# Attention maxima of seven heads: from columns to rows by single-element DMAs instead of matmuls, and a pair of PSUM evacuations on one engine

## The chip, the cores and the metric

One Trainium2 chip, of which the kernel uses one core. The metric is the device time of one execution in microseconds, as the median of several runs.

## What is computed

One layer for a prompt of 1024 tokens and a sample of 64 tokens that follow a cache of 256; the model is 1024 wide and all numbers are float32. After an input projection there are two groups of heads: eight attention heads, 64 wide, whose scores carry a sum of log-forget values, and four heads, 128 wide, with a gated linear recurrence. Both are gated, joined, projected to the output and normalised. The attention of one head:

```
s = einsum('bqhd,bkhd->bhqk', q, k) * 64 ** -0.5
s = s + (c_q[..., :, None] - c_k[..., None, :])      # c = cumsum(logf)
s = where(mask, s, -inf)
p = softmax(s, axis=-1)                              # subtracts each query's maximum
return einsum('bhqk,bkhd->bqhd', p, v)
```

The subtraction of the maximum inside the softmax is where the change lies.

## The kernel before

Matrix products run in a 32-bit format with fewer mantissa bits (`fp32r`), so each operand is split into a high and a low part, and a product is made of two or three.

**Stages.** In the trace the start (projection of the values and of the forget gate) takes the first 81 us. From 81 to 337 us the eight attention heads are worked one after another, here numbered 0 to 7 in their order (four pairs, `s` = 0 and 1 within a pair). Between their steps stands the "filler": projections of later stages, cut into pieces, which `merge` deals out by estimated cost (ratio `RA`). From 337 to 600 us the recurrence runs, again with projections between its steps, and from 600 us the output projection. TensorE (PE) does the matmuls, ScalarE (ACT) exponentials and copies, VectorE (DVE) maxima, masks and subtractions, GpSimd (POOL) low parts, and SyncE (SP) issues nearly all DMAs, in one queue in order.

**One head.** The 1024 queries are worked in two chunks of 512. For a block of 128 keys `scores` makes two matmuls into one bank of PSUM (L811, L812): the first of `QX` and `KX`, the second of `QY` and `KY`, whose extra rows carry the forget sums and the negated maximum. ACT takes the exponential twice (L817, L818), DVE subtracts for the low part (L819), and `values` multiplies with V (L836, three matmuls). The sample of 64 queries is worked in `attend_sample` between the steps of the second chunk.

**The maximum as a row.** The maximum of each query must stand in rows 2 and 3 of a small block of `QY` (high and low part), since the queries are columns there. `prepare` makes all that for the next head while the current one is worked. `max_prep` multiplies queries and keys once more into a bank of tag "tp" (L768), DVE reduces along the free axis (L770 to L774), and `max_columns` writes the negated high and low part into columns 2 and 3 of `mxs[c]`, a tile of 128 queries x 4 query tiles x 4 (L742, L743). Columns 0 and 1 are ones. `put_rows` then turns columns into rows: one matmul with the identity for each tile of 128 queries (L751), 4 for a chunk and 1 of 64 for the sample, into another "tp" bank, and a copy by ACT of the four rows into `QY` (L753). Chunk 0, chunk 1 and the sample have an `mxs` and a `put_rows` each.

**The order.** `prepare` yields 26 pieces for a head. 24 of them are dealt out over the previous head's two chunks by `interleave`; the last two (`put_rows` of chunk 1 and of the sample) come at the start of the head's own chunk 0 (`N_LATE` = 2). The tile scheduler orders each engine's instructions by this emission and its own estimates. DMAs on SP take one of eight semaphores in turn, and each waits for the landing of the DMA that had it before. The weight loads (`wr`, L161) are split into parts by ACT (L171) and POOL or DVE (L172). For a head with `s` = 1 of a later pair, a DMA from `KY` first resets two rows of `QY` (L728); K and Q parts are copied between tiles by DMA at L703 and L735.

**hi_natural.** The recurrence's second inputs come from a projection with 128 tokens to a tile (`nat_unit`, L218). For each tile, ACT scales 128 columns out of PSUM (L963) and DVE the other 128 (L964); with `c` = 0 this runs in the attention, with `c` = 1 in the stage of the recurrence, eight tiles each.

Of the kernel before, what the change touches and what calls it, by code (L numbers as in the profile page):

```python
# [2 lines left out]

# [9 lines left out]
AF = mybir.ActivationFunctionType  # L13
ALU = mybir.AluOpType
AX = mybir.AxisListType

P = 128
D = 1024
SEQ = 1024
DEC = 64  # L20
# [42 lines left out]
def f32(ap):  # L63
    return ap.bitcast(F32)
# [3 lines left out]
def tile_fox_hgrn2(  # L68
# [566 lines left out]
    hin, hin_s = {}, {}  # L635
    st_f, st_k, st_q, gates = {}, {}, {}, {}
    with actx:
# [13 lines left out]

        N_K, N_FIRST, N_PREP, N_LATE = 6, 15, 26, 2
        cv_v = cache_v[0, 0].rearrange("(i t) h d -> t i (h d)", t=P)
        kTs, qTs, kcs = {}, {}, {}

# [32 lines left out]
        def halves(s):  # L690
            return slice(64 * s, 64 * s + 64), slice(64 - 64 * s, 128 - 64 * s)

        def k_prep(p_, s, first):
            r, o = halves(s)
            kT, kc = kTs[p_], kcs[p_]
            act.dma_start(f32(KY[s][o.start:o.start + 2, :]), cc[2 * p_ + s, :, :])

            def part(dst, src):
                act.activation(KX[s][r, dst], src, AF.Copy)  # L699
                if first:  # L700
                    act.activation(KY[s][r, dst], src, AF.Copy)
                else:
                    sync.dma_start(f32(KY[s][r, dst]), f32(KX[s][r, dst]))  # L703
                pool.tensor_tensor(KX[s][o, dst], src, f32(KX[s][r, dst]), op=ALU.subtract)  # L704

            part(slice(T, KW), kc[r, :])
            yield 0.0
            for k0 in (0, T // 2):
                ks = slice(k0, k0 + T // 2)
                part(ks, kT[r, ks])  # L710
                yield 0.0
                yield 0.0
# [10 lines left out]
        def q_prep(p_, s, c, first):  # L723
            r, o = halves(s)
            qT = qTs[p_]
            if c == 0 and s and p_ != PAIRS[0]:

                sync.dma_start(f32(QY[s][2:4, :]), f32(KY[s][4:6, 0:T]))  # L728
            cs = (slice(0, 512), slice(512, T))[c]
            act.activation(QY[s][r, cs], qT[r, cs], AF.Copy)  # L730
            yield 0.0
            if first:
                act.activation(QX[s][o, cs], qT[r, cs], AF.Copy)
            else:
                sync.dma_start(f32(QX[s][o, cs]), f32(QY[s][r, cs]))  # L735
            pool.tensor_tensor(QX[s][r, cs], qT[r, cs], f32(QY[s][r, cs]), op=ALU.subtract)
            yield 0.0

        def max_columns(c, mx, tiles, rows):

            ms = mxs[c]
            dve.tensor_scalar(ms[:rows, :tiles, 2], mx, -1.0, None, op0=ALU.mult)  # L742
            dve.scalar_tensor_tensor(ms[:rows, :tiles, 3], mx, -1.0, f32(ms[:rows, :tiles, 2]), op0=ALU.mult,  # L743
                                     op1=ALU.subtract)
# [8 lines left out]
            act.activation(QY[s][o.start:o.start + 4, c * 512:c * 512 + n], pb[:4, :n], AF.Copy)  # L753
            yield 60.0 * tiles

        def max_prep(s, c):

            qy, ky = QY[s], KY[s]
            rows = Y0[s]
            mx = a2.tile([P, 8], F32, tag="mx", name=nm("mx"))  # L760
            for piece in range(c + 1):
                for i in range(4):
                    qs = slice(c * 512 + i * P, c * 512 + (i + 1) * P)
                    k0 = piece * 512
                    diag = piece == c
                    n = (i + 1) * P if diag else 512
                    pb = bank("tp")
                    pe.matmul(pb[:, :n], qy[rows, qs], ky[rows, k0:k0 + n], start=True, stop=True)  # L768
                    if diag:
                        dve.tensor_tensor_reduce(pb[:, :n], pb[:, :n], cmask[:, 512 - n:512], 1.0,  # L770
                                                 mx[:, 4 + i:5 + i] if c else NEG, ALU.add, ALU.max,
                                                 mx[:, i:i + 1])
                    else:
                        dve.tensor_reduce(mx[:, 4 + i:5 + i], pb[:, :n], axis=AX.X, op=ALU.max)  # L774
                    if diag and i == 3:
                        max_columns(c, mx[:, 0:4], 4, P)
                    yield max(n / 2.4, 107)

        def sample_max(s):
            ns = PAST + DEC  # L780
            mx = a2.tile([P, 8], F32, tag="mx", name=nm("mx"))
            pb = bank("tp")
            pe.matmul(pb[:DEC, :ns], QY[s][Y0[s], SEQ:T], KY[s][Y0[s], SEQ:KW], start=True, stop=True)
            dve.tensor_tensor(pb[:DEC, :DEC], pb[:DEC, :DEC], cmask[:DEC, 384:384 + DEC], op=ALU.add)
            dve.tensor_reduce(mx[:DEC, 0:1], pb[:DEC, :ns], axis=AX.X, op=ALU.max)
            max_columns(2, mx[:DEC, 0:1], 1, DEC)
            yield 140

        def prepare(p_, s, first=False):

            rest = max_prep(s, 1)
            steps = [k_prep(p_, s, first), q_prep(p_, s, 0, first), max_prep(s, 0), q_prep(p_, s, 1, first), islice(rest, 2),
                     put_rows(0, s, 4, P), rest, sample_max(s), put_rows(1, s, 4, P), put_rows(2, s, 1, DEC)]
            if first:
                steps[4:6] = steps[5:3:-1]
            steps.insert(1 if first else 8, v_prep(p_, s))
            for g in steps:
                for x in g:
                    yield x
# [109 lines left out]
        def attention():  # L909
            heads = [(p_, s) for p_ in PAIRS for s in range(2)]  # L910
            yield ("need", ("k", PAIRS[0]))
            fill.debt = 0.0
            first = prepare(PAIRS[0], 0, True)
            for k in range(N_FIRST):
                if k == N_K:
                    yield ("need", ("q", PAIRS[0]))
                next(first)
                yield PREP_FILL
            for i, (p_, s) in enumerate(heads):
                if s == 0:  # L920
                    mixF[p_] = base.tile([P, T], F32, tag="N", name=f"mixF{p_}", bufs=NBUF)
                nxt = iter(())
                n = 0
                if i + 1 < len(heads):
                    p1, s1 = heads[i + 1]
                    if p1 != p_:
                        yield ("need", ("q", p1))
                    nxt, n = prepare(p1, s1), N_PREP - N_LATE
                smp = attend_sample(p_, s)
                if i == 0:  # L930
                    a, b = pieces(first, N_PREP - N_FIRST), pieces(nxt, n)
                else:
                    a, b = pieces(nxt, min(n, PREP_FIRST)), pieces(nxt, max(0, n - PREP_FIRST))
                    a[1:1] = pieces(late, N_LATE)
                late = nxt
                b[4:4] = pieces(smp, 2)
                b[9:9] = pieces(smp, 1)
                for x in interleave(chunk_main(p_, s, 0), a, 7):
                    yield x
                for x in interleave(chunk_main(p_, s, 1), b, 15):  # L940
                    yield x
            while queue:
                yield values()

        def hi_natural(c, w, *lows):

            hin_s[c] = base.tile([DEC, 256], F32, tag="his", name=nm("his"), bufs=2)
            for q in range(2):
                hin[2 * c + q] = base.tile([P, SEQ], F32, tag="N", name=nm("hi"), bufs=NBUF)
            width = 256 + V0 * (c == 0)  # L950
            for i, rows, _ in tok_tiles:
                for cost, pb in nat_unit(w, i, rows, width):
                    yield cost
                r = rn[:rows, i:i + 1]
                if i == NT:
                    lo = low_rows(pb, width, *lows)
                    dve.tensor_tensor(lo[:], pb[:DEC, :width], lo[:], op=ALU.add)
                    act.activation(hin_s[c][:], lo[:, 0:256], AF.Copy, scale=r)
                    if c == 0:
                        act.activation(vs[0][:, 0:V0], lo[:, 256:width], AF.Copy, scale=r)  # L960
                        store_v(0)
                    return
                act.activation(hin[2 * c][:, i * P:(i + 1) * P], pb[:rows, 0:P], AF.Copy, scale=r)  # L963
                dve.tensor_scalar(hin[2 * c + 1][:, i * P:(i + 1) * P], pb[:rows, P:2 * P], r, None, op0=ALU.mult)  # L964
                if c == 0:
                    dve.tensor_scalar(vnat[0][:, i * P:i * P + V0], pb[:rows, 256:width], r, None, op0=ALU.mult)

# [639 lines left out]
```

## Time and profile before

| | |
|---|---|
| median of 3 runs | 717.82 us (717.80, 717.82, 719.88) |
| profiled execution | 718.27 us |
| its span in the trace | 716.4 us (1.87 us lie around it) |
| granted clock of PE | 0.998 |
| PE busy | 702.6 us, 98% of the span |
| ACT, DVE, POOL busy | 325.9, 453.3, 172.5 us |
| SP's DMAs in hardware queue 1 | 23228 packets, 50.18 MB |

How to read it: durations of matmuls overlap, so what one costs PE is read from the distance between starts. In a group's row the numbers behind the bar are its busy time in microseconds, the mean of one in nanoseconds, and the idle time of the engine just ahead of it with what ended it. In a timeline a row has start, duration, engine, line, operation, output and inputs with their shapes, and in brackets the idle time ahead. `SPq` is the issue of a DMA by SP, not its transfer.

### The profile page before, as it was taken

Reading aid. Unit: us, or ns where it says so; the run is one execution under the profiler, and the core shown is the slowest. Engines: PE = TensorE matmul, PEld = TensorE weight load, DVE = VectorE, ACT = ScalarE, POOL = GpSimd, SP = SyncE. Lnnn points to the kernel's source line nnn. Section 1 sums busy time; section 2 is a strip of 40 time slices with the busy share of each in tenths; the row PEclk is TensorE's granted clock in tenths of the full one; section 3 lists DMA queues with packets and bytes.
Section 4 is the critical chain, followed back from the end, with each engine's and each line's share of the span. In section 5 each row is a group of like instructions: output and inputs, shape, how many; then the busy total and the mean of one; then the engine's idle time right before and its main releaser. Section 6 shows DMA issues by size and latency. Waiting matters only on the chain.

```text
span 716.4 us, 11803 instructions
## 1 busy us (share of the span) xinstructions
PE 702.6 (98%) x4319; PEld 633.0 (88%) x4319; DVE 453.3 (63%) x1139; ACT 325.9 (45%) x835; POOL 172.5 (24%) x232
## 2 busy tenths in 40 slices
PE   9999999999999999999999999999999999999996
PEld 7889999889898898888999989999999998878885
DVE  4445367666767666665885575654975788853542
ACT  6755454657557476746522331333313333323542
POOL 4044932535254243421000100010000100012432
PEclk9999999999999999999999999999999999999999
DMA  8823321221131112110220100110101113431211
GB/s 315 329 67 113 95 96 28 64 82 31 49 92 48 24 29 82 39 31 11 108 59 30 41 31 1 65 38 30 51 27 46 38 30 105 164 111 43 104 44 59
DMA packets 23461, 51.01 MB, mean 71 GB/s; under 512 B 5622, under 2 KB 8518, under 8 KB 23404
## 3 DMA queue, kind: packets, MB, share of 16 engines
q1 hardware_dynamic: 23228, 50.18, 21.7%
q8 instruction: 34, 0.56, 0.3%
q14 instruction: 23, 0.19, 0.1%
q10 hardware_dynamic: 176, 0.09, 0.1%
HBM read 36.32 MB, written 9.56 MB: 64 GB/s over the span
## 4 chain that ended last, share of the span: by engine, by line
PE 93%; DVE 3%; ACT 2%; issue 1%; DMA 0%; POOLq 0%; DVEq 0%; SPq 0%; POOL 0%; ACTq 0%
PE pj L235 40%; PE pj L1386 13%; PE av L836 6%; PE pj L218 5%; PE st L811 3%; PE tp L768 2%; PE st L812 2%; PE pj L446 2%; PE st L446 2%; PE tp L446 2%; PE av L446 2%; PE st L1198 2%; PE st L1277 1%; PE pj L212 1%; PE pj L1380 1%; PE st L1137 1%
## 5 line engine op out<-in xcount | busy, mean ns | idle before, releaser
L235 PE MATMUL pj<-hT,whi 128*128 128x364 f32 (+1 forms) x1152 | 213.9, 331 | 0.0
L235 PEld LDWEIGHTS pj<-hT,whi 128*128 128x128 f32 x1152 | 192.5, 188 | 5.3 <-issue 1.0
L235 PE MATMUL pj<-hT,wlo 128*128 128x364 f32 (+1 forms) x576 | 109.2, 329 | 0.0
L235 PEld LDWEIGHTS pj<-hT,wlo 128*128 128x128 f32 x576 | 97.4, 188 | 2.6
L819 DVE TENSOR_TENSOR pl<-st,ph 128x512 fp32r<-128x512 f32 (+1 forms) x96 | 53.3, 556 | 42.3 <-ACT st L818 40.3
L817 ACT ACTIVATE ph<-st 128x512 fp32r<-128x512 f32 (+1 forms) x96 | 47.0, 490 | 70.9 <-DVE st L814 47.5
L108 POOL TENSOR_SCALAR rr<-ss 128x4 f32<-128x4 f32 (+1 forms) x12 | 2.3, 191 | 276.4 <-ACT og L1312 276.1
L1386 PE MATMUL pj<-hT,mx 128*128 128x512 f32 (+1 forms) x264 | 56.3, 374 | 0.0
L1386 PEld LDWEIGHTS pj<-hT,mx 128*128 128x128 f32 x264 | 46.2, 188 | 10.0
L171 ACT ACTIVATE whi<-wr 128x256 fp32r<-128x256 f32 (+1 forms) x112 | 38.5, 407 | 31.4 <-PE pj L235 16.3
L172 POOL TENSOR_TENSOR wlo<-wr,whi 128x256 fp32r<-128x256 f32 (+1 forms) x52 | 37.0, 739 | 57.0 <-ACT whi L171 22.1
L818 ACT ACTIVATE st<-st 128x512 f32<-128x512 f32 (+1 forms) x96 | 46.5, 484 | 0.0
L811 PE MATMUL st<-QX,KX 128*128 128x512 f32 (+1 forms) x96 | 35.3, 368 | 2.8 <-DVE pl L819 2.7
L218 PE MATMUL pj<-whi,hT 128*128 128x264 f32 (+1 forms) x256 | 36.8, 285 | 0.5 <-DVE hi L964 0.4
L1386 PE MATMUL pj<-hT,mxp 128*128 128x512 f32 x144 | 36.4, 402 | 0.0
L218 PEld LDWEIGHTS pj<-whi,hT 128*128 128x128 f32 x256 | 34.0, 188 | 2.2 <-DVE hi L964 0.6
L704 POOL TENSOR_TENSOR KX<-kT,KX 64x544 fp32r<-64x544 f32 x16 | 21.7, 1356 | 54.5 <-ACT KX L699 45.9
L836 PE MATMUL av<-ph,VH 128*128 128x512 f32 (+1 forms) x96 | 34.4, 359 | 0.2 <-ACT ph L817 0.2
L812 PE MATMUL st<-QY,KY 68*128 68x512 f32 (+3 forms) x96 | 33.3, 347 | 0.0
L836 PE MATMUL av<-pl,VH 128*128 128x512 f32 (+1 forms) x96 | 33.1, 345 | 0.0
L836 PE MATMUL av<-ph,VL 128*64 128x512 f32 (+1 forms) x96 | 32.3, 336 | 0.0
L1386 PEld LDWEIGHTS pj<-hT,mxp 128*128 128x128 f32 x144 | 26.2, 188 | 6.1 <-issue 0.3
(307 smaller groups left out, 1324.8 us busy)
## 6 DMA issues: line engine op xcount, KB each, us to landing
wr<-in_w_t_dram SPq DMA_DIRECT2D x24, 512.0 KB
x<-in_xT_dram SPq DMA_DIRECT2D x16, 272.0 KB
xn<-in_x_prompt_dram SPq DMA_DIRECT2D x8, 512.0 KB
wo_raw<-in_w_out_dram SPq DMA_DIRECT2D x8, 512.0 KB
yp<-in_x_prompt_dram SPq DMA_DIRECT2D x6, 512.0 KB
out_dram<-yp SPq DMA_DIRECT2D x12, 256.0 KB
out_dram<-kT SPq DMA_DIRECT2D x4, 544.0 KB
wv<-in_w_v_dram SPq DMA_DIRECT2D x8, 256.0 KB
```

The source lines that it names most:

```text
L171: act.activation(hf[:, cs], raw[:, cs], AF.Copy)
L172: self.eng.tensor_tensor(lf[:, cs], raw[:, cs], f32(hf[:, cs]), op=ALU.subtract)
L218: pe.matmul(pb[:rows, :width], a[:, j, t0:t0 + rows], w[j // 4][b][:, j % 4, :], start=(g == 0 and j == 0), stop=(g == 2 and j == 7))
L235: pe.matmul(pb[:, :n], w[:, j, :], h[:, j, t0:t0 + n], start=(g == 0 and j == 0), stop=(g == 2 and j == 7))
L446: pe.matmul(pb[:, :WV], x[:, j, t0:t0 + P], w[:, j, :], start=(j == 0 and a == 0 and b == 0), stop=(j == 7 and a == 1))
L811: pe.matmul(st[:, :n], kx[:, ks], qx[:, qs], start=True, stop=False)
L812: pe.matmul(st[:, :n], ky[YM[s], ks], qy[YM[s], qs], start=False, stop=True)
L817: act.activation(ph[:, :n], st[:, :n], AF.Exp)
L818: act.activation(st[:, :n], st[:, :n], AF.Exp)
L819: dve.tensor_tensor(pl[:, :n], st[:, :n], f32(ph[:, :n]), op=ALU.subtract)
L836: pe.matmul(av[mm, cols], w[:, b, :], x[:, :n], start=(b == 0 and w is VH[s] and x is ph), stop=(b == nblk - 1 and w is VL[s]), skip_group ...
L1386: pe.matmul(pb[:rows, :n], mx[:, a, j, :rows], wo[b][:, j0 + j, c0:c0 + n], start=(g == 0 and j == 0), stop=(g == 2 and j == nj - 1))
```

## The change

Two edits.

1. For heads 1 to 7 `put_rows` is gone. `rows_by_dma` issues, right where `max_columns` has written a chunk's columns, a DMA for each tile of queries and each of columns 2 and 3, which writes 128 single elements of a column (64 for the sample) along a row of `QY`. That is 8 + 8 + 2 = 18 DMAs a head on SP, 126 in all. The rows of ones are not written again. Head 0 still uses `put_rows`. `prepare` has 23 pieces for the other heads, all dealt out over the previous head, and `v_prep` stands ahead of the second chunk's maxima instead of near the end.
2. In `hi_natural` with `c` = 1, ACT makes both evacuations.

```
+        def rows_by_dma(c, s, tiles, rows):
+            o = halves(s)[1]
+            for i in range(tiles):
+                c0 = c * 512 + i * P
+                for z in range(2, 4):
+                    sync.dma_start(f32(QY[s][o.start + z:o.start + z + 1, c0:c0 + rows]),
+                                   f32(mxs[c][:rows, i, z:z + 1]))
...
                     if diag and i == 3:
                         max_columns(c, mx[:, 0:4], 4, P)
+                        if not first:
+                            rows_by_dma(c, s, 4, P)
...
             max_columns(2, mx[:DEC, 0:1], 1, DEC)
+            if not first:
+                rows_by_dma(2, s, 1, DEC)
...
-            rest = max_prep(s, 1)
-            steps = [k_prep(p_, s, first), q_prep(p_, s, 0, first), max_prep(s, 0), q_prep(p_, s, 1, first), islice(rest, 2),
-                     put_rows(0, s, 4, P), rest, sample_max(s), put_rows(1, s, 4, P), put_rows(2, s, 1, DEC)]
+            steps = [k_prep(p_, s, first), q_prep(p_, s, 0, first), max_prep(s, 0, first), q_prep(p_, s, 1, first),
+                     max_prep(s, 1, first), sample_max(s, first)]
             if first:
-                steps[4:6] = steps[5:3:-1]
-            steps.insert(1 if first else 8, v_prep(p_, s))
+                steps[4:4] = [put_rows(0, s, 4, P)]
+                steps += [put_rows(1, s, 4, P), put_rows(2, s, 1, DEC)]
+            steps.insert(1 if first else 4, v_prep(p_, s))
...
-                    a[1:1] = pieces(late, N_LATE)
-                late = nxt
...
                 act.activation(hin[2 * c][:, i * P:(i + 1) * P], pb[:rows, 0:P], AF.Copy, scale=r)
-                dve.tensor_scalar(hin[2 * c + 1][:, i * P:(i + 1) * P], pb[:rows, P:2 * P], r, None, op0=ALU.mult)
+                if c:
+                    act.activation(hin[2 * c + 1][:, i * P:(i + 1) * P], pb[:rows, P:2 * P], AF.Copy, scale=r)
+                else:
+                    dve.tensor_scalar(hin[2 * c + 1][:, i * P:(i + 1) * P], pb[:rows, P:2 * P], r, None, op0=ALU.mult)
```

**How the order changes.** In the rows below, the words before `<-` name the tile written, those behind it the tiles read; `x8` is eight alike in a row; the changed kernel's lines are numbered up to 13 higher, or 1 lower. First PE, at the first scores of head 1 (`av_1168` still belongs to head 0), with the two pieces held back, before:

```order
L811 MATMUL st_1391<-QX_679,KX_677 128x512
L812 MATMUL st_1391<-QY_543,KY_541 128x512
L751 MATMUL tp_1404<-ident,mxs_547 4x128 x4
L836 MATMUL av_1168<-ph_1318,VH_544 128x256
L836 MATMUL av_1168<-pl_1319,VH_544 128x256
L836 MATMUL av_1168<-ph_1318,VL_680 64x256
L751 MATMUL tp_1413<-ident,mxs_548 4x64
```

and the same place in the changed kernel:

```order
L823 MATMUL st_1403<-QX_679,KX_677 128x512
L824 MATMUL st_1403<-QY_543,KY_541 128x512
L848 MATMUL av_1168<-ph_1319,VH_544 128x256
L848 MATMUL av_1168<-pl_1320,VH_544 128x256
L848 MATMUL av_1168<-ph_1319,VL_680 64x256
```

The small matmuls are gone and nothing stands in their place on PE. The score of the second chunk comes later in the same row and waits there for eight DMAs.

On SP, the queue round the preparation of heads 1 and 2, before (`KY` and `QX` are the copies of K and Q, `wr` the weight loads):

```order
L703 DMA KY_540<-KX_676 64x256
L860 DMA cvn<-in_cache_v_dram 128x2x64
L703 DMA KY_540<-KX_676 64x544
L735 DMA QX_678<-QY_542 64x512
L703 DMA KY_540<-KX_676 64x544
L161 DMA wr_1525<-in_w_t_dram 128x1024
L735 DMA QX_678<-QY_542 64x576
```

and in the changed kernel:

```order
L702 DMA KY_540<-KX_676 64x256
L872 DMA cvn<-in_cache_v_dram 128x2x64
L702 DMA KY_540<-KX_676 64x544
L761 DMA QY_543<-mxs_546 1x128x1 x8
L734 DMA QX_678<-QY_542 64x512
L702 DMA KY_540<-KX_676 64x544
L761 DMA QY_543<-mxs_547 1x128x1 x8
L761 DMA QY_543<-mxs_548 1x64x1 x2
L160 DMA wr_1545<-in_w_t_dram 128x1024
L734 DMA QX_678<-QY_542 64x576
```

The weight load and the second copy of Q have come to stand behind ten more element DMAs.

On ACT, late in head 5, with the splits of two weight blocks (`whi`), exponentials (`ph`, `st`) and small copies, before:

```order
L171 ACTIVATE whi_3255<-wr_2553 128x256 x4
L719 ACTIVATE VH_544<-vnat_91 128x8x64
L225 COPY lowr_3248<-pj_3205 64x264
L817 ACTIVATE ph_3235<-st_3231 128x256
L818 ACTIVATE st_3231<-st_3231 128x256
L699 ACTIVATE KX_677<-kT_1984 64x544
L696 DMA KY_541<-cc 2x1344
L958 ACTIVATE his_2621<-lowr_3248,rn 64x256
L960 ACTIVATE vs_95<-lowr_3248,rn 64x8
L817 ACTIVATE ph_3278<-st_3274 128x128
L818 ACTIVATE st_3274<-st_3274 128x128
L817 ACTIVATE ph_3293<-st_3289 128x512
```

and in the changed kernel:

```order
L170 ACTIVATE whi_3191<-wr_2620 128x256 x4
L718 ACTIVATE VH_544<-vnat_91 128x8x64
L224 COPY lowr_3184<-pj_3167 64x264
L829 ACTIVATE ph_3208<-st_3205 128x512
L830 ACTIVATE st_3205<-st_3205 128x512
L968 ACTIVATE his_2695<-lowr_3184,rn 64x256
L970 ACTIVATE vs_95<-lowr_3184,rn 64x8
L698 ACTIVATE KX_677<-kT_2010 64x544
L170 ACTIVATE whi_3460<-wr_3201 128x256
L829 ACTIVATE ph_3234<-st_3230 128x512
L830 ACTIVATE st_3230<-st_3230 128x512
L170 ACTIVATE whi_3460<-wr_3201 128x256 x3
```

The next weight block's split (`whi_3460`) follows the last one after seven rows, ahead of the exponential `ph_3234`; before, the next (`whi_3362`) came after seventeen rows.

More of the change, by code (lines that the diff above doesn't have):

```diff
@@ L1 @@
 from contextlib import ExitStack
-from itertools import islice
 import concourse.bass as bass
@@ L650, in tile_fox_hgrn2 @@
         Y0 = (slice(0, 66), slice(0, P))
-        N_K, N_FIRST, N_PREP, N_LATE = 6, 15, 26, 2
+        N_K, N_FIRST, N_ALL, N_PREP = 6, 15, 26, 23
         cv_v = cache_v[0, 0].rearrange("(i t) h d -> t i (h d)", t=P)
@@ L754, in put_rows, with max_prep @@
             yield 60.0 * tiles
-        def max_prep(s, c):
+        def rows_by_dma(c, s, tiles, rows):
[5 more added lines that the diff above has]
+                                   f32(mxs[c][:rows, i, z:z + 1]))
+        def max_prep(s, c, first):
             qy, ky = QY[s], KY[s]
@@ L776, in max_prep, with sample_max @@
                         max_columns(c, mx[:, 0:4], 4, P)
+                        if not first:
+                            rows_by_dma(c, s, 4, P)
                     yield max(n / 2.4, 107)
-        def sample_max(s):
+        def sample_max(s, first):
             ns = PAST + DEC
@@ L927, in attention @@
                         yield ("need", ("q", p1))
-                    nxt, n = prepare(p1, s1), N_PREP - N_LATE
+                    nxt, n = prepare(p1, s1), N_PREP
                 smp = attend_sample(p_, s)
                 if i == 0:
-                    a, b = pieces(first, N_PREP - N_FIRST), pieces(nxt, n)
+                    a, b = pieces(first, N_ALL - N_FIRST), pieces(nxt, n)
                 else:
                     a, b = pieces(nxt, min(n, PREP_FIRST)), pieces(nxt, max(0, n - PREP_FIRST))
-                    a[1:1] = pieces(late, N_LATE)
-                late = nxt
                 b[4:4] = pieces(smp, 2)
```

## The prediction

> **What bounds the kernel now.** I read the page's shares first, then its chain of waits, then the busy time stage by stage.
>
> ```profile
> PE 702.6 (98%) x4319; PEld 633.0 (88%) x4319; DVE 453.3 (63%) x1139; ACT 325.9 (45%) x835; POOL 172.5 (24%) x232
> PE 93%; DVE 3%; ACT 2%; issue 1%; DMA 0%; POOLq 0%; DVEq 0%; SPq 0%; POOL 0%; ACTq 0%
> ...
> 81.00:337.00 256.00, 251.85 (x1561) 225.85 (x1560) 171.93 (x465) 152.67 (x355) 100.40 (x98) 1.00 0.18 51
> 337.00:600.00 263.00, 262.52 (x1816) 250.68 (x1815) 183.15 (x447) 83.97 (x248) 11.93 (x21) 1.00 0.14 43
> ```
>
> The columns of a window are its length, then the busy time of PE, weight load, DVE, ACT and POOL, the granted clock, the DMA share and GB/s. The attention of the eight heads runs from 81 to 337 us, and PE is busy in 251.85 of these 256 us at a granted clock of 1.00; the recurrence follows with 262.52 of 263. So PE sets the time in both stages that the change touches. Work taken off PE there is returned one for one, as long as no new wait arises; work taken off ACT or DVE is returned only where PE waits for it.
>
> **Removed from PE.** Next I read the groups of matmuls by shape in the attention, and the timeline round two of them.
>
> ```profile
> L751 PE MATMUL tp<-ident,mxs 128*4 128x128 f32 x64 | 6.4, 223 | 0.5 <-DVE mxs L743 0.3 <-DVE mx L774 0.2
> L751 PE MATMUL tp<-ident,mxs 64*4 64x64 f32 x8 | 1.5, 190 | 0.5 <-DVE mxs L743 0.5
> ```
>
> ```profile
> 174.12 0.39 PE L811 MATMUL st<-QX,KX 128*128 128x512 f32 x1
> 174.35 0.39 PE L812 MATMUL st<-QY,KY 68*128 68x512 f32 x1
> 174.58 0.40 PE L751 MATMUL tp<-ident,mxs 128*4 128x128 f32 x4
> 174.82 0.45 PE L836 MATMUL av<-ph,VH 128*128 128x512 f32 x1
> ...
> 160.56 0.19 PE L751 MATMUL tp<-ident,mxs 64*4 64x64 f32 x1
> 160.68 0.45 PE L811 MATMUL st<-QX,KX 128*128 128x384 f32 x1
> ```
>
> Of the 72 matmuls, seven heads' share goes: 56 wide and 7 narrow ones. Durations overlap, so I don't multiply them (56 x 223 + 7 x 190 ns would be 13.8 us); I take the distance from start to start. Four wide ones hold PE from 174.58 to 174.82, 0.24 us, and a narrow one from 160.56 to 160.68, 0.12 us. The narrow one's first load costs something ahead of it too; I take 0.2. The sum is 14 x 0.24 + 7 x 0.2 = 4.8 us (with 0.12 for the narrow: 4.2).
>
> PE also waits ahead of these matmuls for the maxima that DVE writes. The answer on line L751 sums it up, and the timeline at 282 us shows the two dearest cases.
>
> ```profile
>   DVE mxs L743: 2.3, 4
>   DVE mx L774: 1.7, 5
> ...
> 282.48 0.40 PE L751 MATMUL tp<-ident,mxs 128*4 128x128 f32 x4 [0.28 <-DVE mxs L743]
> 283.70 0.19 PE L751 MATMUL tp<-ident,mxs 64*4 64x64 f32 x1 [0.53 <-DVE mxs L743]
> ```
>
> That is 4.0 us on both of PE's queues (weight load and matmul) together; a wait is seen on both, so it is worth 1.2 to 2 us of the path, and I take 1.5 for the seven heads. With the row DMAs PE asks for the same maxima only some 8 us later, so this wait goes. What is late next is the row itself, below. PE work and wait together: -6.3 us (-5.4 to -6.8).
>
> **Removed from ACT.** Of the 24 copies L753, 21 go, some 9.4 us.
>
> ```profile
> L753 ACT ACTIVATE QY<-tp 4x512 fp32r<-4x512 f32 x16 | 9.3, 579 | 3.9 <-PE tp L751 3.7
> ```
>
> ACT is busy in 152.67 of the stage's 256 us and PE hardly waits for it; I count 0 (at best -0.4 us, where an exponential now starts 0.58 us sooner).
>
> **Added: 126 single-element DMAs on SP.** Each of the seven heads issues 8 for the first half of the tokens, 8 for the second and 2 for the sample. No transfer of before moves single elements, so issue and landing go by the nearest rows.
>
> ```profile
> 89.38 0.33 SPq L161 DMA_DIRECT2D wr<-in_w_t_dram  x1
> 89.77 0.46 SPq L735 DMA_DIRECT2D QX<-QY  x1
> ...
> 33.64 0.57 SPq L118 DMA_DIRECT2D hgv<-in_hg_vecs_dram  x1
> ...
> 281.41 0.64 SPq L728 DMA_DIRECT2D QY<-KY  x1
> ```
>
> ```profile
> 64.50 0.35 SPq L622 DMA_DIRECT2D cc<-ch  x1
> ...
> 66.37 0.47 ACT L618 ACTIVATE ch<-lr 8x320 fp32r<-8x320 f32 x1 [1.89 <-DMA cc<-ch]
> ```
>
> An issue takes 0.33 to 0.64 us, and the next follows at once (0.39 us from 89.38 to 89.77), without waiting for the landing. The copy of 64 partitions between two SBUF tiles, 0.46, is the nearest kin; the transfer of 128 short pieces (32 bytes each, 0.57) and the one between two rows (0.64) are the upper end. From issue to landing an SBUF copy took 1.87 us (64.50 to 66.37). So d, the distance of two issues, is 0.47 us, and the eight rows of a half are there 7d + 1.9 us after the first issue.
>
> The time they have is told by the first score of the second half. In before's trace, head 7:
>
> ```profile
> 312.29 0.17 DVE L743 SCALAR_TENSOR_TENSOR mxs<-mx,mxs 128x4 fp32r<-128x4 f32 x1
> ...
> 321.26 0.39 PE L812 MATMUL st<-QY,KY 128*128 128x512 f32 x1
> ...
> L742 DVE TENSOR_SCALAR mxs<-mx 128x4 fp32r<-128x4 f32 x16 | 6.4, 400 | 0.2
> L743 DVE SCALAR_TENSOR_TENSOR mxs<-mx,mxs 128x4 fp32r<-128x4 f32 x16 | 5.4, 336 | 0.4
> ```
>
> The maxima were written at 312.46 and the score began at 321.26, 8.8 us of cover. In the new order I counted the columns of all matmuls between the last maximum's score and the waiting score, at the spacing above (512 columns in 0.23 us): 8.5, 9.2, 8.0, 8.0, 9.3, 7.2 and 7.8 us for heads 1 to 7. Of it DVE uses about 1.2 us (a reduction, L742 and L743 at 0.40 and 0.34). The need is 1.2 + 7d + 1.9 = 6.4 us at d = 0.47 and 7.6 at 0.64. So the rows come in time, but by one or two microseconds; at 0.64 head 6 would wait 0.4 us. The rows of the first half have over 13 us, those of the sample 7 to 12. I take +0.5 us (0 to 1.5). If SP's queue is held up ahead of them, the cover is gone; that is the slower rival.
>
> The rule that speaks against this is in the Trainium skill, "DMA: Bandwidth & Descriptors", Bandwidth: transfers should be batched, and those under 64 KB are dominated by descriptors; its section on the anatomy of one DMA gives about 2.0 us fixed to each. Paid one behind another, 8 x 2 us would be 16 us a half, against the rows' 7d + 1.9 = 5.2 us.
>
> Each waiting score now has eight DMAs to wait for, some 63 more waits in all in PE's sequencer; the sequencer is ahead of the array here, so I take +0.3 us (0 to 1).
>
> **Moved: the other DMAs behind them on SP, and what ACT does with them.** Weight loads now stand behind up to ten element DMAs, some 5 us. At most places that is hidden. At one it isn't, I think: late in head 5 the scheduler now packs filler projections together (33,208 columns of them in its second half, 21,120 before), and so puts two weight splits close together in ACT's queue. In before:
>
> ```profile
> 277.58 1.32 ACT L171 ACTIVATE whi<-wr 128x256 fp32r<-128x256 f32 x4
> 278.12 2.83 POOL L172 TENSOR_TENSOR wlo<-wr,whi 128x256 fp32r<-128x256 f32 x4 [3.57 <-ACT whi L171]
> 280.97 0.35 SPq L161 DMA_DIRECT2D wr<-in_w_t_dram  x1
> 287.49 0.42 ACT L171 ACTIVATE whi<-wr 128x256 fp32r<-128x256 f32 x1
> ...
> 362.01 0.33 SPq L161 DMA_DIRECT2D wr<-in_w_t_dram  x1
> ...
> 365.73 1.34 ACT L171 ACTIVATE whi<-wr 128x256 fp32r<-128x256 f32 x4 [1.65 <-DMA wr<-in_w_t_dram]
> ```
>
> POOL gave the buffer back at 280.95, the load went out at 280.97, and with 3.7 us (362.01 to 365.73) it was there at 284.7, 2.8 us before ACT asked for it. In the new order only seven rows, about 3.6 us of ACT, stand between the two splits instead of seventeen. ACT would then ask at 282.5 and wait 2.2 us, with two exponentials queued behind the split, and PE behind them with the values of head 5. I take +2.0 us (0, if PE's filler bridges it, to 3).
>
> **The second part.** Eight evacuations of 344 ns go from DVE to ACT (365 ns each).
>
> ```profile
> L963 ACT ACTIVATE hi<-pj,rn 128x128 f32<-128x128 f32 x16 | 5.8, 365 | 28.3 <-PE pj L218 28.2
> L964 DVE TENSOR_SCALAR hi<-pj,rn 128x128 f32<-128x128 f32 x16 | 5.5, 345 | 7.8 <-ACT hi L963 7.8
> ...
>   PE pj L218: 0.4, 1
> ```
>
> PE waited for them once, 0.4 us. I take -0.2 us (-0.6 to +0.4, since the pair is now one behind the other).
>
> **The sum**, against the profiled execution's 718.27 us (span 716.4 and 1.87 around it): 718.27 - 4.8 - 1.5 + 0.5 + 0.3 + 2.0 - 0.2 = 714.6. The median of the three runs, 717.82, is 0.45 below the profiled one, so the forecast is 714.1 us.
>
> **The rivals.**
> - *The gain in full.* PE's buffers and filler hide all new waits, as in the recurrence, where PE is busy in 262.52 of 263 us though ACT waits there for weights (1.65 us at 365.73). Then 717.82 - 6.3 - 0.2 = 711.3 to 712. Chance 0.18.
> - *Eaten up.* The new order costs as much as it frees: the split waits its full 3 us, rows 1.5, the semaphores 1, and of the old waits 0.5 only moves to the next matmul. Then 717.82 - 5.4 + 5.5 is 718 and, with half of it, 716. Chance 0.23. Against it: filler is at hand at most waits. That the freed PE time isn't returned at all (the matmuls lay in gaps) is part of it; the spacing of 0.24 us between busy neighbours speaks against that.
> - *Rows late, slower.* In each of seven heads PE stops ahead of the second half's first score, because an issue of single elements takes longer than any row above. With the covers listed, the stalls together are the sum of 3.1 + 7d less each cover. Without them the other terms leave -4.2 us; from d = 0.83 us on the stalls eat that up, and from 0.87 the kernel is slower by over 0.3%; at d = 1.0 they are 12.7 us, and the time is 714.1 - 0.5 + 12.7 = 726. For it: 128 separate pieces on a queue of which no row shows such. Against it: the row of 128 pieces, 0.57. Chance 0.10.
> - *One at a time.* The transfers follow each other by landing, 1.9 us each: 1.2 + 8 x 1.9 = 16.4 us a half, 8.1 over the mean cover of 8.3, seven times: 714 + 57 = 771. The pair at 89.38 and 89.77 speaks against it. Chance 0.03. It is what the rule on batching named above would lead to.
>
> The forecast itself has 0.46.
>
> **How the numbers follow.** About 0.3% (2.15 us) is what a measurement of this kernel can tell from no change: faster means under 715.7, slower over 720.0. The forecast's own range is 712.5 to 715.7; with the full gain that makes 0.64 for faster. Eaten up is the 0.23 for the same, and the two late cases the 0.13 for slower. The range goes from 711.0 (the full gain with the best ends) to 719.5; it leaves out nearly only the slower cases.
>
> **What would show it.** In the profile after: PE busy time in the attention lower by more than 4 us, of the 72 matmuls of L751 only the first head's nine left; 126 issues of single elements, their distance 0.4 to 0.6 us; no wait of the second half's first score for QY, or one under 0.5 us in heads 6 and 7; one wait of ACT's split for a weight load of about 2 us near 275 to 285 us, with PE waiting for the exponential behind it. The forecast is wrong if that distance is over 0.83 us, if scores wait for QY in most heads, or if PE's saved time comes back as waits for DVE or ACT elsewhere.

## The result and the profile after

The changed kernel takes 714.68 us (median of 5 runs, 714.4 to 715.03), the kernel before 718.24 in its 5 runs: a ratio of 0.995 with a 95% interval of 0.9937 to 0.9963, so 3.6 us or 0.5% less. The forecast was 714.1 us, from 711.0 to 719.5.

The shares of the page, then the two stages by window (columns as before), of the changed kernel:

```profile
PE 697.9 (98%) x4256; PEld 628.6 (88%) x4256; DVE 451.1 (63%) x1131; ACT 319.8 (45%) x822; POOL 172.7 (24%) x232
...
81.00:337.00 256.00, 250.34 (x1515) 224.08 (x1515) 173.52 (x467) 147.49 (x340) 102.28 (x100) 1.00 0.24 56
337.00:600.00 263.00, 262.92 (x1812) 250.77 (x1811) 183.26 (x443) 83.70 (x251) 9.55 (x19) 1.00 0.12 38
```

PE makes 63 matmuls fewer (4256 against 4319) and is busy 4.7 us less; its idle time, the span of 712.9 less 697.9, has grown from 13.8 to 15.0 us. Together that is the 3.5 us by which the span fell. (Of it 0.3 us belongs to the start: matmuls in the first 8 us come up to 0.8 us earlier or later in the profiles of all these kernels. From the 51st matmul to the end it is 702.4 before and 699.2 after, 3.2 less; where two profiles are "lined up" below, their matmuls are matched one by one in order behind that start, and a place where the times of matched matmuls drift apart is where time was won or lost.)

What PE waits for tells which waits went and which came. Before, in the list of PE's waits (total us, times, longest):

```profile
PE st L811 <- DVE pl L819: 2.7, 5, 1.0
...
PE tp L751 <- DVE mxs L743: 0.8, 2, 0.5
...
PE pj L218 <- DVE hi L964: 0.4, 1, 0.4
...
PE av L836 <- ACT ph L817: 0.2, 1, 0.2
PE tp L751 <- DVE mx L774: 0.2, 1, 0.2
```

and after:

```profile
PE st L823 <- DVE pl L831: 3.3, 11, 0.6
PE av L848 <- ACT ph L829: 1.4, 2, 1.2
...
PE tp L776 <- DMA QY<-KY: 0.5, 1, 0.5
```

Gone are the 1.0 us ahead of the small matmuls and the 0.4 us for the second inputs' evacuation. New are 1.2 us for an exponential, 0.5 us for a DMA from `KY` to `QY`, and 0.6 us more for DVE's subtractions: +0.9 us, near the 1.2 by which the idle time grew.

The single-element DMAs (the profile's summary of their line, durations in ns; the time to landing, in us, is recorded for 19 of the 126), and those of head 6's second half with PE's score that needs them:

```profile
L761 SPq DMA_DIRECT2D QY<-mxs x126: 469/592/1429, 113.8 to 312.9; - x126
...
DMA to landing us min/median/max: 1.7/2.0/3.9
```

```profile
283.92 6.54 SPq L761 DMA_DIRECT2D QY<-mxs  x10
...
290.45 0.39 PE L823 MATMUL st<-QX,KX 128*128 128x512 f32 x1
290.77 0.47 PE L824 MATMUL st<-QY,KY 68*128 68x512 f32 x1
```

Ten issues take 6.54 us, 0.65 us from one to the next, and not the 0.47 that I took; the landing of 2.0 us is the one I took (1.9). The eighth DMA is issued near 288.6 and, with a landing of 2.0 us, is there near 290.6 (an estimate: its own landing is not recorded); the score runs at 290.77, 0.32 us behind its partner instead of 0.23. So the rows have no time to spare in this head.

The place late in head 5, on ACT, POOL and SP, and PE's wait for it:

```profile
270.11 1.34 ACT L170 ACTIVATE whi<-wr 128x256 fp32r<-128x256 f32 x4
...
277.39 0.42 ACT L170 ACTIVATE whi<-wr 128x256 fp32r<-128x256 f32 x1 [2.62 <-DMA wr<-in_w_t_dram]
...
270.79 2.83 POOL L171 TENSOR_TENSOR wlo<-wr,whi 128x256 fp32r<-128x256 f32 x4 [8.52 <-PE pj L211]
...
273.64 0.33 SPq L160 DMA_DIRECT2D wr<-in_w_t_dram  x1
...
278.34 0.50 PE L848 MATMUL av<-ph,VH 128*128 128x512 f32 x1 [1.24 <-ACT ph L829]
```

POOL gives the buffer back at 273.62, the load goes out at 273.64, and ACT stands 2.62 us before it can split the block at 277.39. The exponential behind the split comes late, and PE with it, by 1.24 us. The wait is the one forecast (2.2 us on ACT, 2.0 on PE).

A wait that the forecast did not have is the reset of two rows of `QY`. On SP it stands behind ten single-element DMAs:

```profile
155.34 6.99 SPq L761 DMA_DIRECT2D QY<-mxs  x10
162.39 0.70 SPq L727 DMA_DIRECT2D QY<-KY  x1
...
164.40 0.50 PE L776 MATMUL tp<-KY,QY 128*128 128x128 f32 x2 [0.54 <-DMA QY<-KY]
```

### The profile page after: what moved, and what is told of

It is laid out like the page before. It is cut to its first block, busy times and chain, and to the rows that moved or that the text cites. A ratio compares the mean times of both kernels' runs of the same rounds, so it can differ in the third digit from the quotient of the medians.

```text
span 712.9 us, 11941 instructions
## 1 busy us (share of the span) xinstructions
PE 697.9 (98%) x4256; PEld 628.6 (88%) x4256; DVE 451.1 (63%) x1131; ACT 319.8 (45%) x822; POOL 172.7 (24%) x232
## 4 chain that ended last, share of the span: by engine, by line
PE 90%; ACT 3%; DVE 3%; issue 2%; DMA 1%; POOL 0%; POOLq 0%; DVEq 0%; SPq 0%; ACTq 0%
PE pj L234 39%; PE pj L1399 13%; PE pj L217 6%; PE av L848 5%; PE tp L776 2%; PE st L823 2%; PE st L824 2%; PE pj L445 2%; PE st L445 2%; PE tp L445 2%; PE av L445 2%; PE st L1211 2%; PE st L1290 1%; PE pj L1393 1%; PE st L1150 1%
## 5 line engine op out<-in xcount | busy, mean ns | idle before, releaser
L776 PE MATMUL tp<-KY,QY 66*128 66x128 f32 (+5 forms) x96 | 31.6, 346 | 0.5 <-DMA QY<-KY 0.5
```

## The experiments

Times are medians; each ratio compares a kernel with runs of the kernel before on the same chip. The medians of the kernel before lie between 717.87 and 718.24 us from one such comparison to the next, so a difference of two kernels from different comparisons is uncertain by some 0.4 us.

**The first part alone.** The edit puts DVE's evacuation back:

```
-                if c:
-                    act.activation(hin[2 * c + 1][...], pb[:rows, P:2 * P], AF.Copy, scale=r)
-                else:
-                    dve.tensor_scalar(hin[2 * c + 1][...], pb[:rows, P:2 * P], r, None, op0=ALU.mult)
+                dve.tensor_scalar(hin[2 * c + 1][...], pb[:rows, P:2 * P], r, None, op0=ALU.mult)
```

> The first part of the change alone (rows by DMAs; DVE keeps its half of the second inputs' evacuations). PE's order is word for word that of the changed kernel. Theory (the gain is the 63 matmuls taken off PE): about the changed kernel's time, 714.7 to 715.1 us, at most 0.4 us above it, since PE waited 0.4 us for those evacuations in the kernel before. Rival (a good part of the gain comes from the second part): 716 us or more.

Measured: 715.23 us, ratio 0.9957 (0.9945 to 0.997). Between the two expectations, 0.55 us above the changed kernel. The first part brings the greater share: 2.6 us against its own kernel before.

**The second part alone.** The same lines, the other way, in the kernel before.

> The second part alone, put on the kernel before. Theory: within 0.5 us of the kernel before, 717.7 to 718.5 us. Rival (the second part carries a good part of the gain): 717 us or less.

Measured: 716.86 us, ratio 0.9987 (0.9978 to 0.9996), 1.0 us faster. The theory's size was wrong; it is the rival's. Where it lies, the timeline of before shows on PE and on DVE:

```profile
424.01 1.11 PE L218 MATMUL pj<-whi,hT 128*128 128x256 f32 x8
425.52 1.21 PE L218 MATMUL pj<-whi,hT 128*128 128x256 f32 x8 [0.39 <-DVE hi L964]
```

```profile
423.19 0.75 DVE L1101 TENSOR_TENSOR k<-k,f 128x544 f32<-128x544 f32 x1
423.86 0.70 DVE L1103 TENSOR_TENSOR q<-q,f 128x544 f32<-128x544 f32 x1
424.49 0.71 DVE L1107 TENSOR_TENSOR F<-f 128x544 f32<-128x544 f32 x1
425.13 0.34 DVE L964 TENSOR_SCALAR hi<-pj,rn 128x128 f32<-128x128 f32 x1
```

DVE comes to the evacuation behind three operations of the recurrence. Eight matmuls take 0.95 us there, so the next eight could have begun at 424.96 and began at 425.52. With both evacuations on ACT the two groups run together, as in the changed kernel:

```profile
421.05 2.07 PE L217 MATMUL pj<-whi,hT 128*128 128x256 f32 x16
```

Lined up, the two profiles of this run and of before part by 0.7 us at this place and by 0.1 us elsewhere behind the start. The changed kernel against the first part alone says the same: 0.55 us by the medians, 0.7 by the profiles from the 50th matmul on (699.9 to 699.2). So 0.6 to 1.0 us of the 3.6 are the second part's.

**DMAs added, matmuls kept.** The kernel before, with `rows_by_dma` and without the copy:

```
             for i in range(tiles):
                 pe.matmul(pb[:4, i * P:i * P + rows], ms[:rows, i, :], identr[:rows, :rows], ...)
...
-            act.activation(QY[s][o.start:o.start + 4, ...], pb[:4, :n], AF.Copy)
+            if first:
+                act.activation(QY[s][o.start:o.start + 4, ...], pb[:4, :n], AF.Copy)
```

> The kernel before, with its order of pieces, its 63 small matmuls and their banks of PSUM kept, but their result thrown away for heads 1 to 7: the rows are written by the single-element DMAs, and the 21 ACT copies are gone. So it has the DMAs and the lighter ACT and lacks only what PE gains. Theory (the gain is PE's matmuls and the waits ahead of them): no gain, 717.5 to 720 us. Rival (the gain comes from the ACT copies that went, or from the rows being ready sooner): 714.5 to 716 us.

Measured: 719.85 us, ratio 1.0026 (1.0017 to 1.0035), 2.0 us slower. There is no gain without taking the matmuls away. What the dropped copies on ACT are worth alone this run does not show, since it also has the 126 DMAs, and its waits for the reset, which lay behind ten element DMAs in two heads, are longer than the whole loss:

```profile
PE tp L778 <- DMA QY<-KY: 3.1, 2, 1.8
```

**Half of the DMAs.** Only the high part is sent; the low row keeps older numbers, which are the same for all keys of a query and cancel in the softmax.

```
-                for z in range(2, 4):
+                for z in range(2, 3):
```

> The changed kernel with half of its element DMAs: only the high part of the maximum is sent, 9 DMAs a head; the row of the low part keeps what stood in it, which cancels in the softmax since it is the same for all keys of a query. Theory (the DMAs are hidden but for the reset behind them, 0.54 us, and the weight load that comes late to ACT is late by POOL and not by SP's queue): 0.3 to 0.7 us faster than the changed kernel, 714.0 to 714.4 us. Rival (the queue of DMAs holds weight loads and copies back and eats a part of the gain): 1.5 us faster or more, 713.2 us or less.

Measured: 712.75 us, ratio 0.9926 (0.9914 to 0.9939): 1.9 us faster than the changed kernel by the medians, 1.6 by what each gains on its own kernel before, with the same matmuls. The time lies in the rival's range. The reset's wait has gone from the list of waits, but the wait for the exponential late in head 5 has not, and PE's busy time is lower by 1.6 us:

```profile
PE 696.3 (98%) x4256; PEld 628.5 (88%) x4256; DVE 450.8 (63%) x1131; ACT 319.2 (45%) x822; POOL 172.7 (24%) x232
...
PE st L823 <- DVE pl L831: 3.1, 11, 0.6
PE av L848 <- ACT ph L829: 1.4, 2, 1.2
...
158.15 0.72 SPq L727 DMA_DIRECT2D QY<-KY  x1
...
160.83 0.22 PE L776 MATMUL tp<-KY,QY 128*128 128x128 f32 x1
```

Waits of a matmul that are shorter than the tail of the matmul before it show as busy time. Behind five element DMAs the reset goes out at 158.15, 4.2 us earlier than behind ten, and the matmul that waits for it in the changed kernel stands earlier in PE's order and runs without a stop, at 160.83. Lined up, the two profiles part by 1.1 us there, between 161 and 167 us: the changed kernel loses 0.7 us ahead of the matmul at 164.40 (it could have started at 163.70) and the rest in short stops among the next ten. So the late reset costs, with the order round it, twice the 0.54 us that the list of waits shows. At the waiting scores of heads 1, 3, 4 and 6 the profiles part by 0.15 to 0.17 us each; the little that is left is spread, or lies where the order differs (a few dozen rows of PE's order do). So the half of the single-element DMAs costs 1.6 to 2.0 us, the larger part of it by what stands behind them on SP. What the other half costs was not measured.

**The matmuls put back there.** The kernel with half of the DMAs, with `put_rows` for heads 1 to 7 again, its result thrown away:

```
+            if not first:
+                rest = steps[4]
+                steps[4:5] = [islice(rest, 2), put_rows(0, s, 4, P, False), rest]
+                steps += [put_rows(1, s, 4, P, False), put_rows(2, s, 1, DEC, False)]
...
```

> The kernel with only the high parts sent (712.75 us), with the 63 small matmuls and their banks put back for heads 1 to 7, two pieces behind the first half's maxima and at the end of the preparation as before, and their results thrown away: the price of the matmuls, without the late resets that lay over the earlier run of that kind. Theory (63 matmuls hold PE 4.8 us, and the waits ahead of them 0 to 1.5): 717.5 to 719.0 us. Rival (PE's gain came from the order of the pieces or from ACT): under 715 us.

Measured: 718.27 us, ratio 1.0006 (0.9997 to 1.0015), 5.5 us above the kernel without them, as the theory had it. PE is busy 5.9 us longer:

```profile
PE 702.2 (98%) x4319; PEld 632.1 (88%) x4319; DVE 446.1 (62%) x1131; ACT 319.1 (45%) x822; POOL 172.6 (24%) x232
...
PE tp L778 <- DMA QY<-KY: 0.9, 1, 0.9
PE tp L751 <- DVE mxs L743: 0.7, 2, 0.5
```

One late reset of 0.9 us and 0.7 us ahead of the matmuls are among its waits again; the wait for the exponential is nearly gone (0.4 us), and the scores wait 1.5 us for DVE's subtraction instead of 3.1. The scheduler changed PE's order along with them: about 600 of 4,319 rows stand elsewhere. So 5 to 6 us is the price of the 63 matmuls with the order that they bring; a part of it that is the order's alone was not separated. The trace of before prices the matmuls without this: their 21 groups in heads 1 to 7 hold PE from their first start to the start of the next matmul for 14 x 0.24 + 7 x 0.12 = 4.2 us, and they begin 2.1 us later in all than the matmul ahead of them, at 0.23 us for 512 columns, would have let them. Together that is an estimate of 6.3 us.

**Each DMA twice.** First with the copy going to a scratch in DRAM:

```
                 for z in range(2, 4):
+                    sync.dma_start(twin[z - 2:z - 1, c0:c0 + rows], f32(mxs[c][:rows, i, z:z + 1]))
                     sync.dma_start(f32(QY[s][...]), f32(mxs[c][:rows, i, z:z + 1]))
```

> The changed kernel with each single-element DMA sent twice, first to a scratch in DRAM that nobody reads, then to its row: 36 DMAs a head on SP's queue instead of 18. Theory (the rows of the second half come just in time, at 0.65 us from issue to issue as measured in the changed kernel): the last of 16 DMAs lands 1.2 + 15 x 0.65 + 2.0 = 13.0 us after the last maximum's score, against covers of 8.5, 9.2, 8.0, 8.0, 9.3, 7.2 and 7.8 us, so the seven heads stall 33 us in all: 740 to 750 us, with PE waiting ahead of the first score of each second half. Rival (the landings overlap so well, or other work fills in, that the number of DMAs hardly matters): under 720 us.

Measured: 866.23 us, ratio 1.2088 (1.2071 to 1.2106). The direction is the theory's, the size is far off. SP's timeline shows why (then PE's wait, and a window of 50 us):

```profile
113.96 0.54 SPq L762 DMA_DIRECT2D twin<-mxs  x1
...
118.65 0.48 SPq L763 DMA_DIRECT2D QY<-mxs  x1
120.82 0.32 SPq L762 DMA_DIRECT2D twin<-mxs  x1
...
PE st L826 <- DMA QY<-mxs: 94.3, 12, 14.4
...
130.00:180.00 50.00, 34.58 (x166) 31.00 (x167) 20.49 (x51) 18.09 (x42) 13.78 (x14) 0.73 0.38 29
```

After eight element DMAs SP stands from 119.1 to 120.8. Each DMA waits for the landing of the one that had its semaphore eight places before, so the first scratch copy seems to have landed 6.8 us after its issue; the trace records no landing of these DMAs, so this is read from SP's stop alone. A slow landing sets the pace as soon as it is over eight issues (8 x 0.6 = 5 us). The clock fell too, to 0.73 in the window from 130 to 180 us, so not all of the time is DMA.

The second time, the copy goes to SBUF:

```
-                    sync.dma_start(twin[z - 2:z - 1, c0:c0 + rows], ...)
+                    sync.dma_start(twin[r:r + 1, :rows], ...)
```

> As the run with each single-element DMA sent twice, but the copy goes to a scratch in SBUF (one row of 128 elements in a partition of its own) and not in DRAM. Theory (SP issues one DMA after another at 0.65 us, and the landing matters only for the last): the seven heads stall by 33 us in all as worked out before, 740 to 750 us. Rival (the landings set the pace, as each DMA waits for the one that had its semaphore eight places before): near the 866 us of the run with the scratch in DRAM.

Measured: 738.02 us, ratio 1.0268 (1.0243 to 1.0293); 23 us above the changed kernel. SP now issues without a pause, 0.65 us apart, and PE waits in seven scores:

```profile
129.22 0.60 SPq L765 DMA_DIRECT2D QY<-mxs  x1
129.86 0.60 SPq L764 DMA_DIRECT2D twin<-mxs  x1
130.51 0.60 SPq L765 DMA_DIRECT2D QY<-mxs  x1
...
PE st L828 <- DMA QY<-mxs: 16.3, 7, 2.8
```

The number of DMAs is the same as in the run before; the scratch in SBUF instead of DRAM makes 738 us of 866. The mechanism of the slower rival is real, with one wait in each of seven heads. Its waits are half of what I worked out (16 us and not 33): the heads have some 2.4 us more of cover than I gave them, or the changed order of PE (over 100 rows) gave it. That was not separated. The profile is of the fastest run, 733.77 us at a mean granted clock of 0.997; the other three took 737.9 to 739.0 at 0.987 to 0.990, so about 4 of the 23 us go with a lower clock and not with waits of this profile.

**Half loads of the weights.** The two halves of the one buffer are loaded by a DMA each, the first as soon as POOL has worked two of four pieces.

```
+                raw = self.both[:, h * 528:h * 528 + n]
+                sync.dma_start(raw, src[:, h * n:(h + 1) * n])
...
-                raw = wr_.tile([P, src.shape[1]], F32, tag="R", name=nm("wr"))
-                sync.dma_start(raw[:], src)
...
```

> The changed kernel with each weight load cut into two DMAs of half the width into the two halves of the same buffer, so that the first half of the next block is asked for when GpSimd has worked two of the four pieces of the last one. PE's order is that of the changed kernel, word for word. Theory (ACT's wait of 2.6 us for a weight load late in head 5 costs PE its 1.24 us there, and comes from the load that can start only when GpSimd has given the buffer back): the wait of ACT falls under 1.5 us, PE's wait there under 0.5 us, and the time by 0.5 to 1.2 us, to 713.5 to 714.2 us. Rival (the load is late by SP's queue or by the transfer, not by the buffer): no change, or slower by the added DMAs.

Measured: 714.61 us, ratio 0.996 (0.9948 to 0.9972). At the place itself it does what the theory says:

```profile
276.92 0.42 ACT L181 ACTIVATE whi<-wr 128x256 fp32r<-128x256 f32 x1 [0.96 <-DMA wr<-in_w_t_dram]
...
277.87 0.50 PE L861 MATMUL av<-ph,VH 128*128 128x512 f32 x1 [0.45 <-ACT ph L842]
```

So the late load is late by the buffer, and its price on PE falls from 1.24 to 0.45 us. The median does not show it, and misses the expected 713.5 to 714.2: four of the six runs are between 713.96 and 714.71, two near 716.4, and the profile is one of the latter. It shows what was lost there, in the windows and in the timeline of PE:

```profile
290.00:292.00 2.00, 1.33 (x7) 0.96 (x7) 1.05 (x5) 0.45 (x1) 0.79 (x1) 1.00 0.16 30
292.00:293.00 1.00, 0.88 (x9) 0.72 (x8) 0.33 (x1) 1.00 (x3) 0.00 (x0) 1.00 0.94 203
...
294.00:295.00 1.00, 1.00 (x4) 0.81 (x3) 1.00 (x3) 0.95 (x3) 0.00 (x0) 0.50 0.09 1
```

```profile
291.05 0.47 PE L837 MATMUL st<-QY,KY 68*128 68x512 f32 x1 [0.67 <-DMA QY<-mxs]
...
293.42 0.70 PE L836 MATMUL st<-QX,KX 128*128 128x512 f32 x1 [0.53 <-DVE pl L844]
293.91 0.63 PE L837 MATMUL st<-QY,KY 68*128 68x512 f32 x1
294.33 0.63 PE L861 MATMUL av<-ph,VH 128*128 128x512 f32 x1
```

Lined up with the changed kernel, whose PE order is the same, this profile wins 0.8 us at the split and loses 0.75 at head 6's row, which came 0.67 us late: PE had come earlier to a row that was no earlier. DVE then came 0.53 us late, as in the changed kernel, and the granted clock was 0.50 from 293.5 to 297.0: the matmuls of 512 columns follow at 0.42 us instead of 0.23, and some 1.5 us are lost beyond the waits.

**High part only, and no low part computed.** DVE's second operation in `max_columns` is made for head 0 alone.

```
-            dve.scalar_tensor_tensor(ms[:rows, :tiles, 3], mx, -1.0, f32(ms[:rows, :tiles, 2]), ...)
+            if first:
+                dve.scalar_tensor_tensor(ms[:rows, :tiles, 3], mx, -1.0, f32(ms[:rows, :tiles, 2]), ...)
```

> The kernel with only the high parts sent, and the low part not computed either for heads 1 to 7 (15 operations of DVE a pair of heads less by 2: one of 0.34 us a half and one for the sample); what stands in the low row cancels in the softmax. Theory (DVE is ahead of the path except where scores wait for its subtraction, 3.1 us in all): the same as with high parts only, 712.75 us, or up to 1 us faster. Rival (DVE's chain from the last maximum to the rows is on the path in each head): 2 us faster or more, 710.7 us or less.

Measured: 711.35 us, ratio 0.991 (0.9897 to 0.9923), 1.4 us below the kernel with half of the DMAs, between the two expectations. The scores' wait for DVE's subtraction is 2.0 us, 3.1 with half of the DMAs; PE's order is the same, and lined up the two profiles part only at scores, in heads 2, 3, 4 and 6:

```profile
PE st L824 <- DVE pl L832: 2.0, 8, 0.3
```

**Both together.** The last two edits in one kernel.

> Both edits together: only high parts computed and sent, and half loads of the weights. If the two costs lie apart (single-element DMAs in SP's queue and PE's sequencer; the weight load late in head 5), the gains add: 711.3 to 712.2 us, the fastest of all. If the late load came from the element DMAs ahead of it in the queue, half loads bring nothing more: as without them.

Measured: 710.65 us, ratio 0.9898 (0.9885 to 0.9911), the fastest of all and 4.0 us below the changed kernel; the expected 711.3 to 712.2 was too high. By the medians the half loads bring 0.7 us, and the two intervals overlap. The profiles settle it: PE's order is that of the run before, and behind the start the two part at one place alone, by 0.9 us at the late split in head 5 (the wait there falls from 1.2 to 0.3 us). With half of the DMAs, head 6's row no longer takes this gain back.

## Why the prediction was right

The bound was right: PE sets the time, and what is taken off it comes back. Time and range held. That the time is only 0.6 us from the forecast is partly luck, since errors of both signs met in the sum. The terms one by one:

- *PE's matmuls, -4.8 us, and the waits ahead of them, -1.5.* Together -6.3, and right. By the starts in the trace of before it is 4.2 us of hold, 0.6 of lead ahead of the seven narrow ones (0.09 each) and 1.5 of waits. Putting the matmuls back cost 5.5 us of time and 5.9 of PE's busy time, in a changed order. PE's own list of waits shows only 1.0 of the 1.5, since it counts short waits as busy time. The spacing from start to start was the right price: by durations it would have been 13.8.
- *ACT's copies, 0.* Not contradicted, but not shown either: no run takes the copies away alone.
- *Rows late, +0.5, and waits in PE's sequencer, +0.3.* "So the rows come in time, but by one or two microseconds" was worked out with 0.47 us from issue to issue, and it is 0.65, at the upper end of the rows I had and outside the 0.4 to 0.6 that I gave as a sign. With 0.65 and the landing of 2.0 my own sum has head 6 wait 0.55 us; its score was held for 0.09, so the cover was longer than I counted, and the two errors nearly cancel. Half of the DMAs cost some 0.15 us at a score in four heads, near the size of these terms.
- *The DMAs moved behind them.* This is the step that failed: "At most places that is hidden", with a list that had the weight load and not the reset. The reset behind ten element DMAs cost PE 1.1 us in one head. The Trainium skill, in "DMA: Bandwidth & Descriptors" (Bandwidth), calls transfers under 64 KB descriptor-dominated, by measurements of DMAs that GpSimd issued; on SP here the price goes by issues, 0.65 us each for 512 bytes, with a landing of 2.0 us paid once.
- *ACT's split, +2.0.* Right in place and cause: ACT waited 2.6 us (2.2 forecast). On PE it was 1.24 us, so the term was 0.8 too large.
- *The second part, -0.2 (-0.6 to +0.4).* Too small: 0.6 to 1.0 us. I had priced it by the row of PE's wait, 0.4 us; the gap between the starts is 0.56.

The rivals: the gain in full did not come, since 1.2 us for the exponential, 1.1 at the reset and the short waits came. The slower case needed an issue of 0.83 us (0.81, when a head with cover to spare is not counted as a gain); at 0.65 it stayed away, but with 16 DMAs it is there. That transfers go one at a time was wrong for SBUF, and comes near the truth where a landing takes longer than eight issues.

## What to carry to other kernels

Price work that leaves a pipelined engine by the distance of starts, and price DMAs in a queue by their issues (here 0.65 us each for 128 single elements), with everything that stands behind them in that queue on the list. A row of maxima needs no low part, since what is subtracted cancels: sending half was worth about half as much again as the change itself. An evacuation put on the engine that has the other one can be worth more than its length of 0.34 us, where the first engine's queue holds other work: here about 0.7 us at the one place of eight where it did.

## What the runs showed of the hardware

A short stop of PE can cost more than itself. In the profile with half loads PE's waits ahead of the fall were 0.67 and 0.53 us, yet the granted clock fell to 0.50 for 3.4 us and cost about 1.5 us more. The Trainium skill, in "TensorE: Matmul & The Clock Gate" (Part 1, on the clock gate), has the clock fall to half after at least one idle window of about 3.4 us. Here PE was busy 2.22 of the 3.42 us ahead of it (290.13 to 293.55), so the measurement speaks for a lower bar. What the bar is, these runs don't show: in the changed kernel's profile PE was busy 2.18 of 3.42 us (276.43 to 279.85, with the wait of 1.24 us in it), and the clock held.

With a scratch in DRAM, SP could go on only 6.8 us after the issue of a DMA of single elements; the DMAs to SBUF landed after 2.0, and SP did not stop.
